# Reciprocal square roots of the norms: one GpSimd power in place of ten VectorE instructions

## The chip, the core and the metric

The kernel runs on one core of a Trainium2 chip. A core has TensorE (matmuls; the trace shows its weight loads apart, as PEld), VectorE (DVE), ScalarE (ACT), GpSimd (POOL) and a sync engine (SP), which here issues nearly all the DMAs. Each engine works through its own instructions in the order in which they stand in the program, and waits on semaphores for the others. The metric is the device time of one execution in microseconds (us).

## What is computed

Two transformer blocks are applied to 256 latent tokens of 1024 features, the second together with 256 context tokens, in float32. Block 1 has an mLSTM branch, a window attention branch and a convolved feed-forward. Block 2 has two layers: layer 0 with an SSD branch and a retention branch for both streams, then a gated feed-forward for both; layer 1 with latent attention over both streams and a feed-forward for the latent tokens. Every layer begins with a norm, and several branches end in one:

```python
def rmsnorm(x, g):
    xf = x.astype(jnp.float32)
    y = xf * lax.rsqrt(jnp.mean(xf * xf, axis=-1, keepdims=True) + EPS)
    return (y * g.astype(jnp.float32)).astype(x.dtype)

# merge of the mLSTM heads
hn = h * lax.rsqrt(jnp.mean(h * h, axis=-1, keepdims=True) + EPS)
```

The change is about the `rsqrt` of these norms alone. What goes into it is small: one number for each token (and for each head, where a norm is over a head).

## The kernel before, in words

Activations lie with the features on the 128 partitions and 256 tokens along the free dimension, so a stream of 1024 features is eight tiles of 128x256. A float32 product is made of three matmuls (`mm3`, lines 289 to 291): each operand is split into a rounded high part and a remainder, and high-high, high-low and low-high are summed in PSUM. The weights come by DMA (`load_w`, line 263); ScalarE makes the high part (`wh`, line 274), VectorE or GpSimd the remainder (`wl`, line 277). GpSimd does it for the lane "f" and for half of the weights of one phase.

There are three lanes: "m" (main), "f" (fill) and "a" (side). Each has its own buffers and PSUM banks, and the lane's letter ends a tile's name: `t_smm` is a tile of small numbers of lane m, `t_wlf` a weight remainder of lane f, `t_ppa` a PSUM bank of lane a. `t_held` is one large tile in which everything that lives long has its columns.

The order of the instructions on each engine isn't the order of the code: a scheduler, which has a cost for every instruction, sets it for the whole program when the program is built. Priorities (`soon`) put some instructions first where they are ready.

A norm over features (`rms_bc`, line 457) goes through four engines. ScalarE squares the eight tiles and VectorE adds them up. TensorE sums over the partitions with a column of ones (line 467), which leaves the sums of 256 tokens as 128x2 in PSUM. VectorE makes mean plus epsilon of it (line 470) and then calls `rsqrt` (line 225). TensorE spreads the result over the partitions by a product with the identity (line 476), and VectorE multiplies the tiles by it (line 520, or 837 at the very end).

`rsqrt` has ten VectorE instructions on a tile of 128x2 or 128x8, each of which needs the one before: an estimate by integer arithmetic on the number's bits (line 229), and three times the Newton step of lines 231, 232 and 233.

It is called 22 times: 15 times by `rms_bc` (128x2), for the merge of the mLSTM heads (128x8; the result is used at line 998 and by the matmul of line 999), for the SSD norm of both streams (128x2; lines 1447 and 1452) and four times for the group norm of the retention heads (128x8; lines 1525 and 1531).

Of the kernel before, what the change touches and what calls it, by code (L numbers as in the profile page):

```python
# [12 lines left out]
I32 = mybir.dt.int32  # L13
# [6 lines left out]
T = 256  # L20
# [4 lines left out]
NKEEP = 5464  # L25
# [23 lines left out]
# ---------------------------------------------------------------- column pack  # L49
# [22 lines left out]
def ap_of(base, dims, spread=0):  # L72
    """The first partitions of base with other free dimensions; spread: on so many partitions the same."""
    part = (0, spread) if spread else tuple(base.ap[0])
    return bass.AP(base.tensor, base.offset, [part] + [tuple(d) for d in dims])


def cl(ap):
    """List of the columns of a [128, n] tile."""
    return [ap[:, i:i + 1] for i in range(ap.shape[-1])]  # L80
# [10 lines left out]
def weave(a, b, na=1, nb=1):  # L91
    """Emit na steps of a, then nb steps of b, and so on, until both are done."""
# [20 lines left out]
def pipelined(first, second, n, ahead=1):  # L113
    """first(0..ahead), then second(i) behind first(i + ahead)."""
# [11 lines left out]
class Lane:  # L126
    """Slots of one strand of work; w: the lane whose weight slots and PSUM banks it uses."""
# [14 lines left out]
    def halves(self, n):  # L142
        """n wide hi/lo blocks, and slots(j) for norm_mod: their j-th halves."""
# [18 lines left out]
class Kern:  # L162
# [12 lines left out]
    # ------------------------------------------------------------ allocation  # L175
# [8 lines left out]
    def soon(self, n=None):  # L184
        """Instructions that go first where they are ready."""
        return self.tc.high_priority(SOON if n is None else n)
# [4 lines left out]
    def keep(self, *shape):  # L191
        """[128, *shape] columns that live to the end."""
# [10 lines left out]
    # ------------------------------------------------------------ constants  # L203
    def setup(self):
# [5 lines left out]
        nc.vector.memset(self.ones, 1.0)  # L210

# [12 lines left out]
    # ------------------------------------------------------------ small math  # L224
    def rsqrt(self, L, v, n, out=None):
        nc = self.nc
        y = out if out is not None else L.sm(n)
        t = L.sm(n)
        nc.vector.tensor_scalar(y.bitcast(I32), v.bitcast(I32), -0.5, float(0x5F3759DF), op0=MUL, op1=ADD)
        for _ in range(3):  # L230
            nc.vector.tensor_mul(t, y, y)
            nc.vector.scalar_tensor_tensor(t, t, -0.5, v, op0=MUL, op1=MUL)
            nc.vector.scalar_tensor_tensor(y, t, 1.5, y, op0=ADD, op1=MUL)
        return y

    def log1p_exp_neg_abs(self, L, x, out, n):
        """out = log(1 + exp(-|x|))"""
# [24 lines left out]
    # ------------------------------------------------------------ weights  # L262
    def load_w(self, L, src, n, unit):
        """Load [128, n] weights; returns w(i) -> (hi, lo) views of the i-th unit columns."""
# [28 lines left out]
    def proj_fm(self, L, W, nk, h, blocks, evac, k0=0, mw=P, lag=1):  # L293
        """Feature-major product: out[m-block][feature, token].  W: [blocks, 128, nk*mw].  evac may return
        a function, which is called behind the products of the lag-th block after."""
# [19 lines left out]
    def proj_tm(self, L, W, nk, n, h, evac):  # L315
        """Token-major product: out[token chunk][token, n].  W: [128, nk*n]."""
# [18 lines left out]
    # ------------------------------------------------------------ adaptive norm parameters  # L335
    def cond_silu(self, name):
        """silu of the conditions, repeated to 32 columns for each feature block."""
# [10 lines left out]
    def ada_first(self, W, cond, bcol, mid, use):  # L348
        """Shift and scale of block 1's mixer, [128, cond, 4] each, handed to use(half of the features, shift, scale)."""
# [25 lines left out]
    def ada(self, W, cond, bcol, out, groups):  # L375
        """out[p, cond, 48]: columns of silu(cond) @ W + b; a group is 8 blocks of 128."""
# [14 lines left out]
    def ada_rows(self, name, n, behind):  # L391
        """silu of n conditions along the free dimension, on every partition; loaded behind a column's writing."""
# [12 lines left out]
    def ada_dve(self, WT, first, rows, blocks, n, bcol, out, pool=lambda i, c: False, behind=lambda: None):  # L405
        """As ada, by rows of the transposed weights, which begin with block first; n(i): conditions of block i;
# [1515 lines left out]
```

## Time and profile before

| | us |
|---|---|
| median of three runs | 1589.98 |
| the three runs | 1586.48, 1589.98, 1597.94 |
| span of the profiled execution | 1588.7 |

Of the profiled execution the profile gives no other time than its span, from its first instruction to its last. That is 1.3 us under the median of the runs. The granted clock is TensorE's clock as the chip let it run, 1.00 being the higher of its two levels (2.4 GHz) and 0.50 the lower (1.2 GHz); its mean over the span is 0.977.

A timeline row gives start, duration, engine, line, operation, output from inputs with their shapes, how many instructions it merges, and in brackets the idle time of the engine before it and what ended it.

### The profile page before, as it was taken

How to read it: one execution, taken by the hardware profiler on the slowest of the kernel's cores; microseconds unless marked ns; L12 is line 12 of the kernel's file. 1: busy time of each engine (PE TensorE's matmuls, PEld its weight loads, DVE VectorE, ACT ScalarE, POOL GpSimd, SP SyncE). 2: the span in 40 equal slices, each digit the busy share in tenths (PEclk: the TensorE clock that was granted, in tenths of full speed). 3: DMA queues.
4: the chain of work that ended last, by engine and by line, in shares of the span. 5: the costliest groups of instructions: out<-in, count | busy, mean ns of one | idle time of the engine just before them, and what ended most of it. 6: DMA issues, size and time to landing. Idle time of an engine off the chain costs nothing.

```text
span 1588.7 us, 28469 instructions
## 1 busy us (share of the span) xinstructions
PE 1509.1 (95%) x10518; PEld 1331.2 (84%) x10518; DVE 1178.0 (74%) x2589; ACT 789.0 (50%) x1703; POOL 371.2 (23%) x350
## 2 busy tenths in 40 slices
PE   6799989999999998998899999999998999999997
PEld 3598876889999987888899888888897875899997
DVE  4367578579999967887875347988677786688786
ACT  3344546565545455644455323322355556566563
POOL 0102125233231163376453101101001112000000
PEclk9799999999999999999899999999999999999999
DMA  9855742446777763334255235687532340255663
GB/s 321 272 184 198 235 160 67 122 171 228 254 237 248 257 209 135 120 98 133 67 161 159 93 110 182 207 281 277 189 120 93 101 152 1 80 178 183 185 186 107
DMA packets 81387, 268.50 MB, mean 169 GB/s; under 512 B 9056, under 2 KB 10720, under 8 KB 80992
## 3 DMA queue, kind: packets, MB, share of 16 engines
q1 hardware_dynamic: 80672, 266.16, 51.5%
q8 instruction: 82, 1.34, 0.3%
q10 hardware_dynamic: 576, 0.52, 0.1%
q14 instruction: 57, 0.47, 0.1%
HBM read 265.60 MB, written 1.05 MB: 168 GB/s over the span
## 4 chain that ended last, share of the span: by engine, by line
PE 81%; DVE 10%; DMA 5%; issue 2%; ACT 2%; POOL 0%; SPq 0%; DVEq 0%; ACTq 0%; POOLq 0%
PE t_ppm L289 18%; PE t_ppm L290 18%; PE t_ppm L291 18%; PE t_ppf L289 4%; PE t_ppf L291 4%; PE t_ppf L290 4%; DVE t_wlm L277 2%; PE t_ppa L431 2%; PE t_ppm L1648 1%; PE t_ppm L1052 1%; DMA t_wra<-in_wada 1%; PE t_ppf L1063 1%; PE t_ppm L1081 1%; DVE t_junk L421 1%; DMA t_wrm<-in_wup 1%
## 5 line engine op out<-in xcount | busy, mean ns | idle before, releaser
L274 ACT CAST t_whm<-t_wrm 128x512 fp32r<-128x512 f32 (+2 forms) x588 | 345.9, 598 | 403.2 <-PE t_ppm L290 282.3
L277 DVE TENSOR_TENSOR t_wlm<-t_wrm,t_whm 128x512 fp32r<-128x512 f32 (+3 forms) x551 | 401.0, 734 | 149.5 <-ACT t_whm L274 137.4
L289 PE MATMUL t_ppm<-t_g1m,t_whm 128*128 128x256 f32 x952 | 271.2, 290 | 2.2 <-ACT t_g1m L526 0.8
L291 PE MATMUL t_ppm<-t_g1m,t_wlm 128*128 128x256 f32 x952 | 267.5, 285 | 3.0 <-DVE t_wlm L277 3.0
L290 PE MATMUL t_ppm<-t_g1m,t_whm 128*128 128x256 f32 x952 | 269.7, 286 | 0.5 <-POOL t_g1m L523 0.5
L289 PEld LDWEIGHTS t_ppm<-t_g1m,t_whm 128*128 128x128 f32 x952 | 181.2, 192 | 7.9 <-issue 3.9
L291 PEld LDWEIGHTS t_ppm<-t_g1m,t_wlm 128*128 128x128 f32 x952 | 181.6, 192 | 5.9 <-DVE t_wlm L277 4.2
L290 PEld LDWEIGHTS t_ppm<-t_g1m,t_whm 128*128 128x128 f32 x952 | 182.7, 192 | 3.2 <-issue 2.1
L277 POOL TENSOR_TENSOR t_wlf<-t_wrf,t_whf 128x512 fp32r<-128x512 f32 (+1 forms) x92 | 121.9, 1337 | 196.0 <-ACT t_whf L274 138.1
L421 DVE SCALAR_TENSOR_TENSOR t_junk<-t_wra,t_sc 128x1024 bf16<-128x1024 f32 x120 | 151.5, 1265 | 16.7 <-DMA t_wra<-in_wada 15.7
L290 PE MATMUL t_ppm<-t_h8m,t_whm 128*128 128x512 f32 (+1 forms) x448 | 159.8, 358 | 1.9 <-DVE t_h8m L529 1.9
L289 PE MATMUL t_ppm<-t_h8m,t_whm 128*128 128x512 f32 (+2 forms) x448 | 159.4, 358 | 1.1 <-ACT t_h8m L528 1.1
L291 PE MATMUL t_ppm<-t_h8m,t_wlm 128*128 128x512 f32 (+1 forms) x448 | 159.9, 358 | 0.0
L274 ACT CAST t_whf<-t_wrf 128x512 fp32r<-128x512 f32 (+2 forms) x148 | 82.8, 573 | 103.3 <-PE t_ppf L290 71.5
L291 PE MATMUL t_ppm<-t_part,t_wlm 128*128 128x258 f32 (+1 forms) x400 | 113.3, 283 | 0.0
L289 PE MATMUL t_ppm<-t_part,t_whm 128*128 128x258 f32 (+1 forms) x400 | 113.0, 283 | 0.0
L290 PE MATMUL t_ppm<-t_part,t_whm 128*128 128x258 f32 (+1 forms) x400 | 112.9, 282 | 0.0
L291 PE MATMUL t_ppm<-t_g2m,t_wlm 128*128 128x256 f32 x352 | 99.1, 284 | 0.4 <-DVE t_wlm L277 0.4
L290 PE MATMUL t_ppm<-t_g2m,t_whm 128*128 128x256 f32 x352 | 99.0, 282 | 0.0
L289 PE MATMUL t_ppm<-t_g2m,t_whm 128*128 128x256 f32 x352 | 99.0, 282 | 0.0
L290 PEld LDWEIGHTS t_ppm<-t_h8m,t_whm 128*128 128x128 f32 x448 | 84.0, 188 | 15.5 <-DVE t_h8m L529 2.3
L289 PEld LDWEIGHTS t_ppm<-t_h8m,t_whm 128*128 128x128 f32 (+1 forms) x448 | 83.5, 188 | 15.0 <-ACT t_h8m L528 1.3
(550 smaller groups left out, 3553.9 us busy)
## 6 DMA issues: line engine op xcount, KB each, us to landing
t_wrm<-in_wup SPq DMA_DIRECT2D x132, 512.0 KB, 4.1
t_wra<-in_wada SPq DMA_DIRECT2D x102, 512.0 KB, 4.9
t_wrm<-in_w_fm SPq DMA_DIRECT2D x30, 512.0 KB, 3.8
t_wra<-in_wada20t SPq DMA_DIRECT2D x24, 512.0 KB, 4.6
t_wrf<-in_w_fm SPq DMA_DIRECT2D x20, 512.0 KB, 5.1
t_wrf<-in_wd SPq DMA_DIRECT2D x24, 384.0 KB, 3.8
t_wrm<-in_win_fm SPq DMA_DIRECT2D x17, 512.0 KB, 3.7
t_wrm<-in_wdown SPq DMA_DIRECT2D x16, 512.0 KB, 4.5
```

The lines of the kernel that those rows point to most:

```text
L274: nc.scalar.copy(hi[:, :c1 - c0], raw[:, c0:c1])
L277: eng.tensor_sub(lo[:, :c1 - c0], raw[:, c0:c1], hi[:, :c1 - c0])
L289: mm(ps, ah, bh, start=start, stop=False)
L290: mm(ps, ah, bl, start=False, stop=False)
L291: mm(ps, al, bh, start=False, stop=stop)
L421: nc.vector.scalar_tensor_tensor(self.tile([P, D], BF16, "junk", 1), raw, 1.0, rows[:, c], op0=MUL, op1=MUL, accum_out=out[:, c, i:i + 1])
L431: self.nc.tensor.matmul(ps[32 * c:32 * c + 32, :T], cond[:, 32 * k:32 * (k + 1)], raw[:, c * T:(c + 1) * T], start=k == 0, stop=k == 7, ti ...
L1052: nc.tensor.transpose(pp[:, j * T + t * P:j * T + (t + 1) * P], Ps[t][:, c * P:(c + 1) * P], self.m["ident"])
L1063: nc.tensor.matmul(po[j * 64:(j + 1) * 64, :T], v[j][c], pts[j][c // 2][:, (c % 2) * T:(c % 2 + 1) * T], start=c == 0, stop=c == 3, tile_p ...
L1081: nc.tensor.matmul(ps, q[:, t * P:(t + 1) * P], kall, start=True, stop=False)
L1648: nc.tensor.matmul(ps, q, K[0:96, hd], start=True, stop=True)
```

## The change

A column block of eight columns of -0.5 is kept (set once by GpSimd), and `rsqrt` becomes one GpSimd `tensor_tensor` with the operation power: `y = v ** -0.5`. Nothing else that is computed changes. Comments and docstrings are taken out of the file as well; with that, a line behind `rsqrt` has a number that is smaller by four in the changed file (476 is 472 there).

```diff
-NKEEP = 5464
+NKEEP = 5472
...
         self.ones = self.keep(P)
         nc.vector.memset(self.ones, 1.0)
+        self.mhalf = self.keep(8)
+        nc.gpsimd.memset(self.mhalf, -0.5)
...
     def rsqrt(self, L, v, n, out=None):
-        nc = self.nc
         y = out if out is not None else L.sm(n)
-        t = L.sm(n)
-        nc.vector.tensor_scalar(y.bitcast(I32), v.bitcast(I32), -0.5, float(0x5F3759DF), op0=MUL, op1=ADD)
-        for _ in range(3):
-            nc.vector.tensor_mul(t, y, y)
-            nc.vector.scalar_tensor_tensor(t, t, -0.5, v, op0=MUL, op1=MUL)
-            nc.vector.scalar_tensor_tensor(y, t, 1.5, y, op0=ADD, op1=MUL)
+        self.nc.gpsimd.tensor_tensor(y, v, self.mhalf[:, :n], op=ALU.pow)
         return y
```

Since the scheduler orders the whole program again, instructions that the diff doesn't touch move too. The first place is TensorE where the latent stream goes from the retention norm and the output product of layer 0 to its feed-forward; it works first for the context stream's norm (lines 467 and 476, in the changed file 463 and 472). Before:

```order
L291 MATMUL t_ppf<-t_g1f,t_wlf 128x256
L467 MATMUL t_ppf<-t_held,t_g1f 128x1
L1511 MATMUL t_ppm<-t_g2m 128x64 x4
L467 MATMUL t_ppf<-t_held,t_g1f 128x1 x3
L476 MATMUL t_ppf<-t_held,t_smf 128x128 x2
L1531 MATMUL t_ppm<-t_held,t_g2m 128x128 x4
L289 MATMUL t_ppm<-t_g1m,t_whm 128x256
```

and now:

```order
L287 MATMUL t_ppf<-t_g1f,t_wlf 128x256
L463 MATMUL t_ppf<-t_held,t_g1f 128x1 x4
L1527 MATMUL t_ppm<-t_held,t_g2m 128x128 x4
L285 MATMUL t_ppm<-t_g1m,t_whm 128x256
...
L287 MATMUL t_ppm<-t_g1m,t_wlm 128x256
L472 MATMUL t_ppf<-t_held,t_smf 128x128 x2
```

The product that spreads the norm's result (472) stood right behind the one that makes its sums, and ahead of the transposes of the retention output (1531, now 1527). It now stands behind the transposes and 24 weight products.

The second place is GpSimd over the same stretch and the norm of the latent stream that follows it, in the changed program (lines 229 are the powers; 273 are weight remainders, 277 before):

```order
L273 TENSOR_TENSOR t_wlf<-t_wrf,t_whf 128x512 x7
L229 TENSOR_TENSOR t_smm<-t_smm,t_held 128x8
L273 TENSOR_TENSOR t_wlf<-t_wrf,t_whf 128x512
L229 TENSOR_TENSOR t_smf<-t_smf,t_held 128x2
L273 TENSOR_TENSOR t_wlm<-t_wrm,t_whm 128x512 x2
L523 TENSOR_TENSOR t_h8m<-t_g1f,t_h8m 128x256 x2
```

The powers stand in GpSimd's one queue among the weight remainders; before, this queue had nothing of the norms' square roots.

The third place is ScalarE where block 1's feed-forward (its gelu at line 820, before 824) overlaps with the SSD branch of the context stream (its exponentials at line 1387, before 1391). Before, one table load stood at the first gelu and the exponentials all ahead of it. Now:

```order
L553 ACTIVATE t_g1m<-t_ppm,t_held 128x256
L820 ACT_TABLE_LOAD
L820 ACTIVATE t_g1m<-t_g1m 128x256
L1389 ACTIVATE t_g2f<-t_held 128x128 x4
L270 CAST t_whm<-t_wrm 128x512
L1387 ACT_TABLE_LOAD
L1387 ACTIVATE t_g2f<-t_ppf 128x512
L270 CAST t_whm<-t_wrm 128x512
L820 ACT_TABLE_LOAD
L820 ACTIVATE t_g1m<-t_g1m 128x256
```

Two exponentials now fall between gelus, so that the table is changed four times more than before (twice here, and twice some 25 rows on).

## Rows read from the trace of the kernel before

**Rows 1.** The page, busy time of each engine, its share, and instructions.

```profile
PE 1509.1 (95%) x10518; PEld 1331.2 (84%) x10518; DVE 1178.0 (74%) x2589; ACT 789.0 (50%) x1703; POOL 371.2 (23%) x350
```

**Rows 2.** The page, chain of work that ended last, by engine.

```profile
PE 81%; DVE 10%; DMA 5%; issue 2%; ACT 2%; POOL 0%; SPq 0%; DVEq 0%; ACTq 0%; POOLq 0%
```

**Rows 3.** Busy times over the span of lines 229, then 233 (instructions in brackets).

```profile
0.00:1588.70 1588.70, 5.77 (x22) 0.98 0.52 169
0.00:1588.70 1588.70, 21.27 (x66) 0.98 0.52 169
```

**Rows 4.** Timeline of TensorE, the products behind a square root.

```profile
221.11 0.46 PE L999 MATMUL t_ppm<-t_g1m,t_g2m 128*128 128x128 f32 x2 [1.76 <-ACT t_g1f L571]
...
730.48 0.46 PE L1452 MATMUL t_ppm<-t_g1m,t_g2m 128*128 128x128 f32 x2 [3.07 <-DVE t_g1m L1447]
...
786.88 1.23 PE L476 MATMUL t_ppf<-t_held,t_smf 128*128 128x128 f32 x4 [2.73 <-DVE t_smf L233]
788.63 1.09 PE L1531 MATMUL t_ppm<-t_held,t_g2m 128*128 128x128 f32 x4 [0.52 <-DVE t_g2m L1525]
...
827.32 1.02 PE L476 MATMUL t_ppm<-t_held,t_smm 128*128 128x128 f32 x4 [2.25 <-DVE t_smm L233]
...
1204.19 0.68 PE L476 MATMUL t_ppf<-t_held,t_smm 128*128 128x128 f32 x4 [2.64 <-ACT t_K L1592]
...
1581.17 0.71 PE L476 MATMUL t_ppm<-t_held,t_smm 128*128 128x128 f32 x4 [2.22 <-DVE t_smm L233]
```

**Rows 5.** Timeline of VectorE, the end of one square root, the last one's input.

```profile
827.10 0.16 DVE L233 SCALAR_TENSOR_TENSOR t_smm<-t_smm 128x2 f32<-128x2 f32 x1
...
1578.99 0.16 DVE L470 TENSOR_SCALAR t_smm<-t_ppm 128x2 f32<-128x2 f32 x1 [1.37 <-PE t_ppm L467]
```

**Rows 6.** GpSimd's instructions by line and shape: count, busy us, mean ns, idle before.

```profile
L277 POOL TENSOR_TENSOR t_wlf<-t_wrf,t_whf 128x512 fp32r<-128x512 f32 x84 | 115.9, 1390 | 156.2 <-ACT t_whf L274 99.0 <-PE t_ppf L291 19.3 <-ACT t_whm L274 16.1
...
L414 POOL COPY t_wra<-t_g1m 128x1 f32<-128x1 f32 x8 | 3.1, 401 | 6.2 <-DVE t_junk L421 3.3 <-issue 2.8
```

**Rows 7.** Timeline of VectorE and GpSimd around an uncovered hand-over between them.

```profile
713.63 0.42 DVE L1423 TENSOR_TENSOR t_g1m<-t_ppm,t_held 128x256 f32<-128x256 f32 x1
...
714.12 0.74 POOL L1425 TENSOR_TENSOR t_g2m<-t_g2m,t_g1m 128x256 f32<-128x256 f32 x1 [1.14 <-DVE t_g1m L1423]
```

**Rows 8.** Timeline of VectorE and GpSimd, at the square roots of rows 4.

```profile
214.43 1.11 DVE L990 TENSOR_SCALAR t_smm<-t_held 128x8 f32<-128x8 f32 x1 [0.62 <-ACT t_g1m L986]
...
214.22 2.71 POOL L277 TENSOR_TENSOR t_wlf<-t_wrf,t_whf 128x512 fp32r<-128x512 f32 x2 [5.87 <-DMA t_wra<-in_wada]
...
723.05 0.17 DVE L1435 TENSOR_SCALAR t_smm<-t_smm 128x2 f32<-128x2 f32 x1 [0.79 <-ACT t_g2m L1433]
...
724.40 2.51 POOL L277 TENSOR_TENSOR t_wlf<-t_wrf,t_whf 128x512 fp32r<-128x512 f32 x2 [2.68 <-ACT t_whf L274]
...
785.57 0.17 DVE L1523 TENSOR_SCALAR t_smm<-t_smm 128x8 f32<-128x8 f32 x1
...
1199.37 0.16 DVE L470 TENSOR_SCALAR t_smm<-t_ppf 128x2 f32<-128x2 f32 x1 [0.25 <-PE t_ppf L467]
```

**Rows 9.** Stretches: from:to, length, busy PE, PEld, DVE, ACT, POOL, granted clock, DMA, GB/s.

```profile
223.40:230.20 6.80, 6.80 (x35) 5.93 (x36) 4.85 (x30) 2.48 (x8) 0.16 (x1) 0.50 0.40 151
732.00:735.40 3.40, 3.40 (x18) 3.40 (x18) 0.31 (x1) 0.98 (x3) 2.52 (x2) 0.50 0.09 37
827.60:831.00 3.40, 3.40 (x18) 3.40 (x18) 2.62 (x7) 1.13 (x3) 0.00 (x0) 0.50 0.27 107
1410.00:1575.00 165.00, 165.00 (x1384) 165.00 (x1383) 128.11 (x257) 101.82 (x190) 12.96 (x10) 1.00 0.58 174
```

**Rows 10.** ScalarE's table load at the gelu, and its high parts of lane m's weights.

```profile
L824 ACT ACT_TABLE_LOAD x1 | 1.3, 1283 | 0.2 <-DVE t_g1m L563 0.2
...
L274 ACT CAST t_whm<-t_wrm 128x512 fp32r<-128x512 f32 (+2 forms) x588 | 345.9, 598 | 403.2 <-PE t_ppm L290 282.3
```

**Rows 11.** Timeline of GpSimd, its first instruction on two tensors.

```profile
32.38 0.72 POOL L527 TENSOR_TENSOR t_g1m<-t_g1m 128x256 fp32r<-128x256 f32 x1 [31.43 <-ACT t_g1m L526]
```

## Prediction

> **What bounds the kernel.** I read the page's busy times first. TensorE is busy for 95% of the span, VectorE for 74%, GpSimd for 23% [rows 1], and of the chain that ended last 81% is TensorE and 10% VectorE [rows 2]. So a VectorE instruction that goes away is worth something only where TensorE stands still for it, and TensorE stands still for 1588.7 - 1509.1 = 79.6 us in all.
>
> Then I asked for the four lines of the square root over the whole span. Line 229 runs 22 times, so there are 22 roots and 220 instructions. Line 233 takes 21.27 us in 66 instructions, a mean of 0.32 us [rows 3], where an undisturbed step takes 0.16 [rows 5]: on average a step is held up as long again. A root is thus at least 10 x 0.16 = 1.6 us long and often several times that.
>
> Third, TensorE's timeline behind each root. At 15 of the 22 TensorE has other work until the root is there. At seven it stands idle just before a product that needs a root; those are the seven rows of [rows 4]: 1.76 us at the mLSTM merge, 3.07 at the latent SSD norm, 2.73 and 0.52 where the context's feed-forward norm and the last retention norm run side by side, 2.25 at the latent feed-forward norm, 2.64 at the first norm of layer 1, 2.22 at the very end. Together 15.2 us: the most that shorter roots can give back directly, 1.0% of the span. (The row at 1204.19 names ScalarE as what it waited for last; the root's chain was the long wait before that.)
>
> Last, the granted clock. After three of these places (the mLSTM merge, the latent SSD norm, the latent feed-forward norm) it falls to 0.50, for 6.8, 3.4 and 3.4 us [rows 9].
>
> **The change, step by step.** *Removed:* 220 VectorE instructions. For 15 roots I cost that at nothing: TensorE's other work hides them, and if that cover goes, what shows is the power's own latency, below.
>
> *Added:* 22 powers on GpSimd. No row shows one. The nearest from below is GpSimd's copy of a single column, 0.401 us; the nearest from above is its subtraction of 512 columns, 1.39 us [rows 6]. A power is more work than a copy, on 2 or 8 columns; I take twice the copy, 0.8 us, for two columns and 1.2 us, most of the way to the upper row, for eight. Nothing in these rows excludes a power that is longer than any of them, and that is the first rival. A hand-over from VectorE to GpSimd costs 714.12 - (713.63 + 0.42) = 0.07 us [rows 7]; from a step's end to TensorE it was 827.32 - 827.26 = 0.06 us [rows 4, 5]. I take 0.07 for each. From the input's start to TensorE's product: 0.16 + 0.07 + 0.8 + 0.07 = 1.1 us.
>
> The Trainium skill (GPSIMD Engine Reference, Engine selection) speaks against the place: element-by-element work belongs on VectorE, since GpSimd is about two times slower on two inputs. The trace agrees in kind, 0.401 us for a copy of one column against 0.16 us for a VectorE step. By that rule alone the power would take some 0.32 us (an estimate: twice that step), still a fifth of ten steps, and the sum below would be 0.5 us lower at the end of the kernel and the same elsewhere.
>
> The seven places:
> - *End.* The sum enters at 1578.99 [rows 5] and the product starts at 1581.17 [rows 4]: 2.18 us become 1.1. Gain 1.1.
> - *First norm of layer 1.* The input is there at 1199.37 + 0.16 [rows 8], the root 0.94 us on, at 1200.5. TensorE's work reached to 1204.19 - 2.64 = 1201.55. Gain 2.6.
> - *Latent feed-forward norm.* TensorE now has 41 rows between the product that makes the sums and the one that spreads the result. A weight product takes 165.00/1384 = 0.119 us [rows 9], so they cover 4.9 us. Gain 2.25.
> - *Latent SSD norm.* Input ready at 723.05 + 0.17; GpSimd idle until 724.40 [rows 8]; root at 724.2, diagonal 0.5 us later. TensorE had work until 730.48 - 3.07 = 727.4. Gain 3.07.
> - *mLSTM merge.* Input at 215.54, GpSimd taken until 216.93 [rows 8], eight columns until 218.2, diagonal until 218.8. TensorE had work until 219.35. Gain 1.76.
> - *Retention norm and context norm.* The mean is there at 785.57 + 0.17 [rows 8]; with 1.2 us of power and 0.7 us for the multiplication behind it, as now, the transposes start at 787.8 in place of 788.63. But the order has moved: the context's spreading product no longer fills part of this wait, it comes 24 products later. So one idle stretch of 3.6 us replaces 2.73 + 0.52. I count 0.
>
> Sum: 1.1 + 2.6 + 2.25 + 3.07 + 1.76 = 10.8 us gained.
>
> *The clock.* At 1.00 a product takes 0.119 us, at 0.50 it took 3.40/18 = 0.189 [rows 9], so 37% of such a stretch is lost. If the three stretches behind gaps that close stay at 1.00, that is 0.37 x 13.6 = 5.0 us. Other idle time of TensorE remains near them; I take 3, with 0 and 5 as bounds.
>
> *Moved, on ScalarE.* Four more table loads of 1.28 us [rows 10], 5.1 us, between casts that TensorE needs. ScalarE waits 403 us in all before these casts, nearly three quarters of it for TensorE to free a buffer [rows 10], so it runs ahead and most is hidden: 0 to 5.1, I take 2. If the cover goes, TensorE waits for the high part of a weight.
>
> *Moved, on GpSimd.* A power can come up while a subtraction of 1.39 us runs [rows 6], or stand behind one whose cast isn't there yet. While the power waits at the queue's head for VectorE, the remainders behind it wait as well, and TensorE for them. And TensorE's cover is thinner: at ten norms 25 to 41 rows now stand between the two products, at an eleventh 15; at nine of these eleven it was more before (up to 61 rows), and 25 rows are 3.0 us. A latency of 1.1 + 1.4 = 2.5 us still fits under that. I take 1.5 us for all of this (0 to 4).
>
> Net: -10.8 - 3 + 2 + 1.5 = -10.3 us, from 1588.7 to 1578.4. The median of the runs is 1.3 us above the profiled span, so the prediction is **1580 us**.
>
> **Rivals.**
>
> *The power is a long routine (slower).* The place is the wait of TensorE's spreading product for GpSimd. For: no row prices a power, and it is unlike the additions and products that GpSimd does here. Against: the tiles have two or eight columns, and even 512 columns of arithmetic take 1.39 us. It decides from about 2.7 us for two columns, where latency passes the 3.0 us of cover. At 5 us, latency 5.3: with 0.119 us a row the eleven norms stand still for 21 us in all, less 5 us of idle time there that two of them had before; the end loses 3 us, the norm of block 1's feed-forward (2 rows of cover) 3, the SSD norm still gains 1.6: +20.4, or 1610 for the median. If eight columns take four times as long, 20 us, the mLSTM merge (root at 216.93 + 20) and the last retention norm lose some 16 and 18 us more: 1644. Chance 0.20, spread over 1592 (at 3 us for either shape) to 1644.
>
> *The new order gives it back (no change).* A whole-program reordering by a table of costs: of TensorE's rows about one in seven stands elsewhere. The bounds above (table loads 5.1, queue 4, clock 0) give -1.7, and a few us of new waits for weights, of the size that are seen now, end at 1585 to 1600. Chance 0.21.
>
> *The clock holds everywhere (faster).* All gains, nothing lost: -10.8 - 5.0, and VectorE, lighter by 220 steps of 0.16 to 0.32 us (35 to 70 us), delivers remainders a little earlier: 1566 to 1574. Chance 0.14.
>
> *The first power waits for code.* GpSimd's first two-input instruction ran at 32.38 [rows 11]; nothing shows that it could have run sooner, and the first norm now needs one earlier. If not, the first norm, its products and the weights behind them shift by up to 18 us, partly under the loads of the start: 1590 to 1608. The Trainium skill (GPSIMD Engine Reference, Instruction dispatch) says that the first call to a freshly loaded kernel pays a load of some 6 us that no instruction shows; by that figure it would be over before the first norm, and no run here shows it yet. Chance 0.05.
>
> **The numbers.** Forecast 0.40 (1574 to 1585). A measurement of this kernel can tell about 1%, 16 us: below 1574 counts as faster, above 1606 as slower. Faster takes the third rival and a little of the forecast's edge: 0.16. Slower takes most of the first rival and a little of the last: 0.20. Within 1%: 0.64. For the range, 1566 to 1612 leaves out the longer half of the slow power and the extreme of the clock case, less than 2 in 10.
>
> **What would show it.** GpSimd rows of line 229, 22 of them, at 0.4 to 1.5 us. The idle time before the spreading products at 1204 and 827 gone, at the end about 1.1 us instead of 2.22; before the transposes of the retention output one gap of about 3.6 us. VectorE's busy time down by 35 to 70 us with TensorE's nearly unchanged. Clock at 1.00 after the latent SSD norm. The prediction is wrong if a power takes over 2.7 us, if GpSimd's queue holds powers back for longer than a subtraction, or if TensorE waits for casts between 340 and 400 us.

## The result, and the profile after

The kernel with the power takes 1575.19 us (median of four runs, 1572.88 to 1576.11), the one before, in runs beside it, 1589.71. The ratio is 0.9896, with a 95% interval from 0.9869 to 0.9922: faster by about 1%, on the border of what the prediction called a change that can be told. The forecast was 1580 with a range from 1566 to 1612. The profiled span went from 1588.7 to 1573.0 us.

First the page of the kernel after, busy times and the chain that ended last. They answer to [rows 1, 2]. Its line numbers are 4 lower than those of before.

```profile
PE 1506.4 (96%) x10518; PEld 1330.7 (85%) x10518; DVE 1133.2 (72%) x2369; ACT 796.1 (51%) x1707; POOL 391.1 (25%) x373
...
PE 78%; DVE 8%; issue 6%; DMA 5%; ACT 2%; POOL 1%; SPq 0%; POOLq 0%; DVEq 0%; ACTq 0%
```

VectorE lost 220 instructions and 45 us. TensorE's work is nearly the same. Its idle time before products, added up from the timeline, fell from 72.8 to 60.1 us; that is 12.7 of the 15.7 us of the span. (The prediction's 79.6 us have the 6.8 us behind the last product as well.)

The new instruction, from GpSimd's groups by line and shape (count, busy us, mean ns, idle before):

```profile
L229 POOL TENSOR_TENSOR t_smm<-t_smm,t_held 128x2 f32<-128x2 f32 x13 | 9.4, 726 | 191.1 <-DVE t_smm L466 185.6 <-DVE t_lgf L242 5.5
L229 POOL TENSOR_TENSOR t_smm<-t_smm,t_held 128x8 f32<-128x8 f32 x3 | 4.9, 1647 | 2.8 <-DVE t_smm L1519 2.5
L229 POOL TENSOR_TENSOR t_smf<-t_smf,t_held 128x8 f32<-128x8 f32 x2 | 3.3, 1638 | 0.0
L229 POOL TENSOR_TENSOR t_smf<-t_smf,t_held 128x2 f32<-128x2 f32 x2 | 1.8, 918 | 0.7 <-DVE t_smf L466 0.7
```

A power of two columns takes 0.70 us where nothing disturbs it, one of eight columns 1.64.

TensorE's timeline at the products that answer to [rows 4] (start, length, line, and in brackets the idle time before and who ended it):

```profile
217.45 0.49 PE L995 MATMUL t_ppm<-t_g1m,t_g2m 128*128 128x128 f32 x2 [0.31 <-DVE t_g1m L994]
...
720.98 0.49 PE L1448 MATMUL t_ppm<-t_g1m,t_g2m 128*128 128x128 f32 x2 [1.56 <-DVE t_g1m L1443]
...
722.21 0.49 PE L1448 MATMUL t_ppm<-t_g1m,t_g2m 128*128 128x128 f32 x2 [0.74 <-DVE t_g1m L1443]
...
775.14 0.83 PE L463 MATMUL t_ppf<-t_held,t_g1f 128*128 128x1 f32 x6 [1.33 <-ACT t_g1f L450]
...
777.90 0.63 PE L1527 MATMUL t_ppm<-t_held,t_g2m 128*128 128x128 f32 x4 [1.93 <-DVE t_g2m L1521]
...
813.01 0.61 PE L472 MATMUL t_ppm<-t_held,t_smm 128*128 128x128 f32 x4
...
1184.90 0.60 PE L472 MATMUL t_ppf<-t_held,t_smm 128*128 128x128 f32 x4
...
1188.16 0.76 PE L285 MATMUL t_ppm<-t_h8m,t_whm 128*128 128x256 f32 x3 [2.66 <-ACT t_h8m L524]
...
1190.80 0.58 PE L286 MATMUL t_ppm<-t_h8m,t_whm 128*128 128x256 f32 x1 [1.88 <-DVE t_h8m L525]
...
1565.81 0.71 PE L472 MATMUL t_ppm<-t_held,t_smm 128*128 128x128 f32 x4 [1.02 <-POOL t_smm L229]
```

The waits at 813 and 1185 are gone, the mLSTM merge waits 0.31 us, the end 1.02. The latent SSD norm still waits 1.56 and 0.74. At the first norm of layer 1 part of the wait has moved on, to the product behind the norm (2.66 and 1.88; it was 1.11 and 1.94 there before).

The granted clock, in stretches of the kernel after (columns as in rows 9):

```profile
608.20:625.30 17.10, 13.59 (x50) 12.00 (x51) 11.63 (x56) 5.53 (x20) 0.00 (x0) 0.50 0.07 27
342.00:345.40 3.40, 3.40 (x10) 1.85 (x9) 3.40 (x8) 3.26 (x7) 1.34 (x1) 0.50 0.85 290
376.10:379.50 3.40, 3.02 (x12) 2.84 (x13) 3.40 (x7) 3.06 (x5) 0.00 (x0) 0.50 0.75 255
778.90:782.30 3.40, 3.40 (x18) 3.40 (x18) 1.30 (x4) 1.52 (x3) 1.07 (x1) 0.50 0.29 117
813.10:816.50 3.40, 3.40 (x31) 3.40 (x30) 2.87 (x8) 2.52 (x7) 3.26 (x3) 1.00 0.51 159
```

0.50 is the lower of the two levels, 1.2 GHz. Behind the latent feed-forward norm the clock now stays at 1.00, as forecast, and so it does behind the mLSTM merge (219.8 to 226.6 us) and the latent SSD norm (722.7 to 726.1). Behind the retention norm (the row at 778.90) half clock went from 10.2 us to 3.4. But other stretches are new or longer: 3.4 us each at 342 and 376 us, at gaps of TensorE that are new, 6.8 us each at 28 and 1284 us, and 17.1 us in place of 6.8 around 615 us. Over the whole span half clock went from 71.6 to 73.9 us.

### The profile page after: what moved, and what is told of

The parts are those of the page before. It is cut to its first block, busy times and chain, and to the rows that moved or that the text cites. A ratio compares the mean times of both kernels' runs of the same rounds, so it can differ in the third digit from the quotient of the medians.

```text
span 1573.0 us, 28294 instructions
## 1 busy us (share of the span) xinstructions
PE 1506.4 (96%) x10518; PEld 1330.7 (85%) x10518; DVE 1133.2 (72%) x2369; ACT 796.1 (51%) x1707; POOL 391.1 (25%) x373
## 4 chain that ended last, share of the span: by engine, by line
PE 78%; DVE 8%; issue 6%; DMA 5%; ACT 2%; POOL 1%; SPq 0%; POOLq 0%; DVEq 0%; ACTq 0%
PE t_ppm L285 17%; PE t_ppm L286 17%; PE t_ppm L287 17%; PE t_ppf L285 4%; PE t_ppf L286 4%; PE t_ppf L287 4%; PE t_ppa L427 2%; PE t_ppm L1644 2%; DVE t_wlm L273 1%; PE t_ppm L1048 1%; PE t_ppf L1059 1%; DMA t_wra<-in_wada 1%; DMA t_wrm<-in_wdown 1%; PE t_ppm L1077 1%; PE t_ppm L972 1%
## 5 line engine op out<-in xcount | busy, mean ns | idle before, releaser
L273 POOL TENSOR_TENSOR t_wlf<-t_wrf,t_whf 128x512 fp32r<-128x512 f32 (+1 forms) x92 | 118.0, 1291 | 193.9 <-ACT t_whf L270 184.2
L287 PE MATMUL t_ppm<-t_h8m,t_wlm 128*128 128x512 f32 (+2 forms) x448 | 159.2, 357 | 0.0
L286 PE MATMUL t_ppm<-t_g2m,t_whm 128*128 128x256 f32 x352 | 98.6, 282 | 0.0
```

The lines of the kernel that those rows point to most:

```text
L273: eng.tensor_sub(lo[:, :c1 - c0], raw[:, c0:c1], hi[:, :c1 - c0])
L286: mm(ps, ah, bl, start=False, stop=False)
L287: mm(ps, al, bh, start=False, stop=stop)
```

## What made a root long

The prediction saw that a step of the old root took 0.32 us on average where an undisturbed one takes 0.16, and left it at that. The reasons stand in the trace of before. This is VectorE's timeline at the latent feed-forward norm, from the input of the root (L470) to the last step but one; the last is in [rows 5].

```profile
819.60 0.16 DVE L470 TENSOR_SCALAR t_smm<-t_ppm 128x2 f32<-128x2 f32 x1 [1.08 <-PE t_ppm L467]
819.79 0.77 DVE L229 TENSOR_SCALAR t_smm<-t_smm 128x2 int32<-128x2 int32 x1
820.60 0.16 DVE L231 TENSOR_TENSOR t_smm<-t_smm 128x2 f32<-128x2 f32 x1
820.80 0.16 DVE L232 SCALAR_TENSOR_TENSOR t_smm<-t_smm 128x2 f32<-128x2 f32 x1
821.00 0.16 DVE L233 SCALAR_TENSOR_TENSOR t_smm<-t_smm 128x2 f32<-128x2 f32 x1
821.07 0.42 DVE L712 SCALAR_TENSOR_TENSOR t_g1f<-t_g1f,t_ppf 128x256 f32<-128x256 f32 x1
821.40 1.27 DVE L231 TENSOR_TENSOR t_smm<-t_smm 128x2 f32<-128x2 f32 x1
822.71 0.67 DVE L232 SCALAR_TENSOR_TENSOR t_smm<-t_smm 128x2 f32<-128x2 f32 x1
823.41 1.21 DVE L233 SCALAR_TENSOR_TENSOR t_smm<-t_smm 128x2 f32<-128x2 f32 x1
824.65 1.20 DVE L231 TENSOR_TENSOR t_smm<-t_smm 128x2 f32<-128x2 f32 x1
825.88 1.18 DVE L232 SCALAR_TENSOR_TENSOR t_smm<-t_smm 128x2 f32<-128x2 f32 x1
```

And GpSimd's in the same stretch:

```profile
817.85 2.69 POOL L277 TENSOR_TENSOR t_wlf<-t_wrf,t_whf 128x512 fp32r<-128x512 f32 x2 [0.26 <-DMA t_wrm<-in_wup]
821.36 1.30 POOL L277 TENSOR_TENSOR t_wlf<-t_wrf,t_whf 128x512 fp32r<-128x512 f32 x1 [0.82 <-ACT t_whf L274]
822.62 0.73 POOL L682 TENSOR_TENSOR t_part<-t_g1f,t_part 128x256 fp32r<-128x256 f32 x1
823.32 3.73 POOL L277 TENSOR_TENSOR t_wlf<-t_wrf,t_whf 128x512 fp32r<-128x512 f32 x3
```

Read the two together. The estimate at 819.79 ends at 820.56, just as the second subtraction of 817.85 ends. Three steps of 0.16 follow while GpSimd rests. The step of 821.40 ends at 822.67, with the subtraction of 821.36; the next ends with GpSimd's addition, and each of the following with one of the three subtractions of 1.24 us. A step that starts while GpSimd works on two tensors waits for the end of GpSimd's instruction. Over the whole span, counted one instruction at a time, 187 of the 220 steps start with GpSimd at rest: they take 0.16 us, and none over 0.17. Of the 33 that start beside a GpSimd instruction, 29 take 0.35 to 1.28 us, and each of these ends 0.02 to 0.03 us after a GpSimd instruction on two tensors. The other four take 0.16: three beside a `MEMSET`, which reads no tensor, and one in the last 0.06 us of a GpSimd product. All waits together are 23.4 us of VectorE. The Trainium skill (SBUF — State Buffer, SBUF: two separate sides) states this: VectorE and GpSimd share one pair of ports under an exclusive lock; a VectorE instruction with two SBUF inputs (against a GpSimd instruction that reads SBUF) or in one of its two-port modes excludes a GpSimd instruction and is excluded by it, and the one that comes second blocks for the whole of the first. The trace agrees for the 25 waiting steps with two inputs and for the three beside a `MEMSET`; four of the 29 are estimates (line 229), which have one input, and no view shows their mode.

GpSimd is not the only cause. VectorE's other instructions stand between the steps in its queue, as the one of line 712 does above. Of the 88.2 us that 21 of the roots took from the input's end to the root's end (all but that of the context's SSD norm), the steps' own 0.16 us make up 33.6, the waits for GpSimd 21.7 and other VectorE instructions about 33. The six roots between 1176 and 1396 us are 27.8 us long and wait for GpSimd for 0.4 us in all.

On GpSimd the root stands in the same queue as the subtractions, so it waits once, for those that stand ahead of it. The same root after:

```profile
808.24 0.16 DVE L466 TENSOR_SCALAR t_smm<-t_ppm 128x2 f32<-128x2 f32 x1 [0.16 <-PE t_ppm L463]
...
810.30 0.69 POOL L229 TENSOR_TENSOR t_smm<-t_smm,t_held 128x2 f32<-128x2 f32 x1
```

It waits 1.9 us, for the rest of one subtraction and the whole of another, and is there 2.6 us after its input, where it was 7.5. From the input's end to the root's end, over all roots but one (that of the context's SSD norm, which ran for 42 us between other work): 88.2 us before, 27.6 after; the median root of two columns 3.85 us before, 0.8 after; of eight columns 5.1 and 1.7. That is some 60 us less; undisturbed (2.0 us against 0.8 and 1.7) they would differ by 21.

## The experiments

All twelve, with the time of each beside the kernel before on the same chip. *Roots* is the sum just told (21 roots, input's end to root's end, from the trace); *middle* is the stretch from the input of the latent SSD root to the product of the latent feed-forward norm, and *its roots* the three roots in it on the latent strand's way (two retention norms, the feed-forward norm). A strand is the work of one stream, here latent or context. These three columns come from one profiled execution of each kernel; the times are medians, and runs of one kernel lie up to 14 us apart (e11).

| kernel | us | ratio, 95% | roots | its roots | middle |
|---|---|---|---|---|---|
| before | 1590 to 1592 | 1 | 88.2 | 17.1 | 104.3 |
| after | 1575.2 | 0.9896 (0.9869 to 0.9922) | 27.6 | 6.0 | 94.8 |
| e1 power in seven | 1587.5 | 0.9974 (0.9959 to 0.9989) | 69.5 | 10.8 | 100.6 |
| e2 power in fifteen | 1585.2 | 0.9960 (0.9945 to 0.9975) | 44.4 | 10.1 | 100.2 |
| e3 one step | 1578.8 | 0.9917 (0.9890 to 0.9944) | 30.1 | 6.5 | 93.4 |
| e4 power twice | 1584.6 | 0.9966 (0.9953 to 0.9980) | 53.0 | 10.1 | 99.9 |
| e5 two steps | 1580.8 | 0.9928 (0.9904 to 0.9952) | 55.8 | 11.9 | 99.2 |
| e6 four steps | 1604.4 | 1.0079 (1.0053 to 1.0105) | 118.3 | 24.3 | 107.8 |
| e7 one root longer | 1591.2 | 1.0006 (0.9986 to 1.0025) | 88.7 | 15.6 | 103.5 |
| e8 exponentials ahead | 1575.3 | 0.9897 (0.9867 to 0.9927) | 27.5 | 6.2 | 94.9 |
| e9 estimate only | 1581.1 | 0.9939 (0.9914 to 0.9965) | 7.2 | 1.8 | 93.8 |
| e10 eights twice | 1588.9 | 0.9993 (0.9978 to 1.0009) | 39.0 | 9.2 | 98.6 |
| e11 eights by Newton | 1587.0 | 0.9973 (0.9950 to 0.9995) | 45.4 | 17.2 | 102.5 |
| e12 power in eights | 1588.5 | 0.9977 (0.9963 to 0.9992) | 70.5 | 10.0 | 99.2 |

**e1 and e2: where the gain sits.** The theory of the prediction (A): only the seven places where TensorE stood idle count.

```diff
+        self.nroot += 1
+        if self.nroot - 1 in (2, 8, 10, 13, 14, 16, 21):   # e2: not in
             self.nc.gpsimd.tensor_tensor(y, v, self.mhalf[:, :n], op=ALU.pow)
+        else:
+            self.newton(L, v, n, y)
```

> The power for the seven roots behind which TensorE stood idle (mLSTM merge, latent SSD norm, last latent retention norm, both feed-forward norms of block 2's layer 0, first latent norm of layer 1, the very end); the ten VectorE steps for the other fifteen. Theory A (the gain is TensorE's idle time behind these seven): nearly all of it stays, 1574 to 1579 us. Rival B (the gain is VectorE's relief, spread over all roots): 7 of 22 of 14.5 us, so 1585. Rival C (the new order as such): no relation to the number, anywhere from 1570 to 1590.

> The reverse: the power for the fifteen roots that TensorE's other work covered, the ten VectorE steps for the seven. Theory A: little gain, 1585 to 1590 us. Rival B: 15 of 22 of 14.5 us, so 1580. Rival C: anywhere from 1570 to 1590.

Measured: 1587.5 and 1585.2. The seven places bring 0.26% (interval 0.11 to 0.41), the fifteen others 0.40% (0.25 to 0.55); which of the two brings more can't be told. A is wrong on e1. In e2 its 1585 to 1590 just holds the 1585.2, but A had the fifteen at next to nothing, and what they bring is clear of noise. B is wrong on e2 (1580); C forecast no number that could fail. TensorE's timeline in e1, at the places and behind them (its lines are 14 higher than after's):

```profile
219.30 0.49 PE L1009 MATMUL t_ppm<-t_g1m,t_g2m 128*128 128x128 f32 x2 [0.33 <-DVE t_g1m L1008]
...
725.45 0.79 PE L1462 MATMUL t_ppm<-t_g1m,t_g2m 128*128 128x128 f32 x2 [3.04 <-DVE t_g1m L1457]
...
777.70 1.44 PE L477 MATMUL t_ppf<-t_held,t_g1f 128*128 128x1 f32 x6 [3.03 <-ACT t_g1f L464]
...
783.10 0.80 PE L299 MATMUL t_ppf<-t_h8m,t_whf 128*128 128x256 f32 x2 [1.20 <-ACT t_h8m L538]
...
786.21 0.58 PE L300 MATMUL t_ppf<-t_h8m,t_whf 128*128 128x256 f32 x1 [2.31 <-DVE t_h8m L539]
...
1575.68 1.22 PE L486 MATMUL t_ppm<-t_held,t_smm 128*128 128x128 f32 x4 [1.02 <-POOL t_smm L231]
```

At the seven places 15.2 us of idle time became 4.4 (0.33, 3.04, 1.02 and nothing at the others): 10.8 us closed, just the sum that was forecast, by coincidence: the latent SSD norm, forecast to close, still waits 3.04, and the retention norm with the context's, put at 0, lost its 3.25. And TensorE's whole idle time fell by 2.0 only, from 72.8 to 70.8. What used to be a wait for the root is now a wait for the tiles before and behind the norm, at 777.70, 783.10 and 786.21. A gap that closes is not a gain by itself.

**e3, e4, e5, e6: the root's length alone.** One, two and four steps in place of three, on VectorE (the edit against the kernel before; e3 is the same, written into the changed file); and the power followed by a second one with exponent 1.

```diff
-        for _ in range(3):
+        for _ in range(1):   # e5: 2, e6: 4
```

```diff
-        self.nc.gpsimd.tensor_tensor(y, v, self.mhalf[:, :n], op=ALU.pow)
+        t = L.sm(n)
+        self.nc.gpsimd.tensor_tensor(t, v, self.mhalf[:, :n], op=ALU.pow)
+        self.nc.gpsimd.tensor_tensor(y, t, self.mone[:, :n], op=ALU.pow)
```

> All roots on VectorE with one Newton step in place of three (4 instructions, less accurate roots), no GpSimd power. Theory A: a root of 4 x 0.16 us, about 0.65 undisturbed, is as short as the power with its hand-overs: 1573 to 1579 us. Rival B: 132 of 220 VectorE instructions go: 60% of 14.5 us, 1581. If only a move to GpSimd helps (VectorE steps are stretched by GpSimd's work): 1582 to 1586.

> Every root as two powers in a row on GpSimd (the second with exponent 1), so 0.7 us longer for two columns and 1.6 for eight, VectorE as in the changed kernel. Theory A: covered roots (eleven with 25 or more rows) show nothing; the end loses 0.7, the last retention norm 1.6, the mLSTM merge 0 to 1.6, the first norm of layer 1 up to 0.7: 1578 to 1581 us. Rival B: VectorE is as light as in the changed kernel, so 1575.

> Two Newton steps in place of three in all 22 roots, all on VectorE, no power (7 instructions per root; the roots are slightly less exact). Theory L (every us that a root is long costs a fixed share, wherever the root stands, since the work that covers it is then missing elsewhere): the time lies on the line through three steps (1591) and one step (1579), so 1585, within 2. Theory S (only the seven places where TensorE stood idle count, 0.5 us each): 1587 to 1588. Theory O (each root length gives another order of the whole program, and the orders differ by several us for no reason of the roots): anything from 1578 to 1596, off the line by more than 3.

> Four Newton steps in place of three in all 22 roots, all on VectorE, no power (13 instructions per root). Theory L: on the same line, 1597, within 2. Theory S: seven places by 0.5 us, 1594 to 1595. Theory O: anything from 1584 to 1602, off the line by more than 3; at or below 1591 would speak for it most plainly.

Measured: 1578.8, 1580.8, 1591 and 1604.4 for one, two, three and four steps; 1584.6 for the power twice. With the steps the time rises, by 2, 10 and 13 us; the 2 are within noise, the other two clear of it. That is no straight line: e5 lies 4 us below L's and e6 7 us above, so L failed in that form, and S (0.5 us at seven places) is far too small for the last two. O had forecast a distance of more than 3 from the line, so an effect of the order stays possible. One step alone, still on VectorE, already has most of the gain; e3 leaves B open (1581 lies in its interval), but e4 doesn't: VectorE is as light there as in the kernel after, and the time is some 10 us longer (0.7%). So the root's length matters, not only the load that VectorE loses. e4 speaks against A and its "nothing" for covered roots as well (1578 to 1581): it makes roots longer by 0.70 us for two columns and 1.64 for eight. It also gives GpSimd some 20 us more work, and no run separates that from the roots' length.

**e7: does an order alone move the time?** One root, where TensorE never waited, gets a fourth step; TensorE's order changes from there on.

```diff
-        for _ in range(3):
+        for _ in range(4 if self.nroot - 1 in (3,) else 3):
```

> The kernel before, with a fourth Newton step in one root alone, that of the norm ahead of block 1's feed-forward, where TensorE did not wait: three more VectorE instructions, 0.5 us, and otherwise the same work; but TensorE's order changes from there on (about a fifth of its rows stand elsewhere). Theory L: 1591 to 1592. Theory S: 1591. Theory O: 3 us or more away from 1591, to either side, which would be the size by which an order alone moves the time.

Measured: 1591.2 beside 1591.1, 0.06% with an interval of 0.2% to either side. Here another order costs nothing that can be seen; its profile still has 3.5 us more idle time of TensorE than before's. This is one other order; what others cost is not shown.

**e8: the four extra table loads.** The context's SSD scores are issued one step ahead, so that no exponential comes between gelus.

```diff
-        yield from pipelined(first, second, 4, 1 if lat else 0)
+        yield from pipelined(first, second, 4, 1 if lat else 1)
```

> The kernel with the power, and the context's SSD scores issued one step ahead of their use (as the latent stream has it already), so that its four exponentials all stand before the first Gelu on ScalarE: three table loads in place of seven, nothing else is computed. If the four loads cost what the prediction took (2 us, bounds 0 and 5.1): 1573, within 1570 and 1575. If the two gaps of TensorE at 339 and 374 us and the two stretches at half clock behind them are all theirs (4.5 us and 2.5 us): 1568. If they are hidden: 1575. Theory O: 3 us or more above 1575 is possible as well.

ScalarE's table loads in the kernel after:

```profile
L820 ACT ACT_TABLE_LOAD x3 | 3.8, 1283 | 2.5 <-DVE t_g1m L559 2.4
L1387 ACT ACT_TABLE_LOAD x2 | 2.6, 1283 | 0.0
```

and in e8 (beside them each kernel has two more, at the start and at the end):

```profile
L820 ACT ACT_TABLE_LOAD x1 | 1.3, 1283 | 2.4 <-DVE t_g1m L559 2.4
```

Two waits of TensorE in this stretch of the kernel after, the second one for an exponential behind a load:

```profile
341.33 1.46 PE L1384 MATMUL t_ppf<-t_g2f,t_held 128*128 128x512 f32 x2 [2.22 <-DVE t_g2f L1381]
...
376.48 1.22 PE L1404 MATMUL t_ppf<-t_g2f 128*128 128x256 f32 x2 [2.31 <-ACT t_g2f L1387]
```

In e8 one wait of 1.28 us is left of the two, neither stretch at half clock is there, and its profiled execution, the fastest of its four runs, is 3.9 us shorter than after's. The medians are 1575.34 and 1575.19, with runs of e8 from 1570.9 to 1579.7. So the loads cost nothing by the medians and some 4 us by the two profiles, which noise alone could make; a version that beats the kernel after isn't shown.

**e9: the integer estimate alone.**

```diff
-        for _ in range(3):
+        for _ in range(0):
```

> The kernel before with no Newton step at all: each root is the integer estimate alone, one VectorE instruction (the three steps that make it exact are left out). From the inputs' ends to the roots' ends the traces so far give, summed over 21 roots (the context's SSD root, which nothing needs at once, left out): 118 us with four steps, 88 before, 56 with two, 53 with the power twice, 30 with one, 28 with one power; the times are 1604, 1591, 1581, 1585, 1579, 1575. Here the sum would be 5 us. Theory L (a fixed share, 0.32 us of time per us of root): 1568, within 3. Theory F (a floor: roots of under 0.8 us are hidden behind TensorE's other products): 1574 to 1576.

Measured: 1581.1, although the roots take 7 us in all. L would have 1568: wrong. A floor (F) is nearer, but its 1574 to 1576 lies below the interval as well (1577 to 1586). Nothing was won here by roots shorter than the power. That they lose against it isn't shown: the intervals of e9 and of the kernel after overlap a little. Nor can the profile say where 6 us would come from, since it is of the fastest of five runs (1575.2; the others 1579.8 to 1581.7) and its span is after's, 1573.0: in it TensorE's idle time is 5.7 us more than after's (65.8 against 60.1) and its busy time 6.1 us less.

**e10, e11, e12: two columns or eight.**

```diff
-        self.nc.gpsimd.tensor_tensor(y, v, self.mhalf[:, :n], op=ALU.pow)
+        if n == 2:   # e12: n == 8
+            self.nc.gpsimd.tensor_tensor(y, v, self.mhalf[:, :n], op=ALU.pow)
+        else:
+            self.newton(L, v, n, y)
```

In e10 the second power of e4 stands behind the five powers of eight columns only.

> The kernel with the power, where the five roots of eight columns are followed by a second power (with exponent 1, so the result stays), and the seventeen of two columns are as they were. The five get longer by 1.64 us and a hand-over each, 8 to 12 us in all. Theory L: 1578 to 1579. If these five are covered (all but the last retention norm have other products beside them): 1575 to 1576. If they are what made the kernel with all powers doubled slow: 1582 to 1585.

> The power for the seventeen roots of two columns, the integer estimate and three Newton steps on VectorE for the five of eight columns. Alone a power of eight columns (1.64 us) is as long as ten VectorE steps; between other VectorE work the ten steps took 5.1 us in the median before. If that is what counts, the five get 13 us longer than with the power: theory L 1579. If only the instructions' own length counts: 1575. If VectorE's lower load is part of the gain: 1576.

> The reverse of the run before: the power for the five roots of eight columns alone (the mLSTM merge and the four retention norms), the estimate and three Newton steps on VectorE for the seventeen of two columns. Over the kernels so far the time goes with the summed length of the eight-column roots (from the input's end to the root's end, 10 us with the power, 24 before, 31 in the run before this) more than with that of the two-column roots (18 and 64): a plane through twelve of them gives 0.64 and 0.14 us of time per us, within 3. Theory E (the eight-column roots are the path, the others mostly covered): 1575 to 1578 if they are all of it, 1583 by that plane. Theory L (length counts alike everywhere, 0.25): 1587. Theory P (gains of parts don't add, since a shorter root in one strand leaves the other strand's in its place): 1585 to 1588, as the other partial kernels.

Measured: 1588.9, 1587.0 and 1588.5. No theory of e10 (1575 to 1585) or of e11 (1575 to 1579) had these times. Five roots of eight columns that are 13.6 us longer in all take back the whole gain (e10); all 22 made longer cost less in e4, though the two profiled spans are the same, 1587.1. Of the 14.1 us between the spans of e10 and after, 9.2 lie ahead of the middle stretch. If the five roots were the path, the power for them alone should bring most of the gain. It brings 3.3 us (e12): E is wrong; P (1585 to 1588) and L (1587) both agree with the interval (1586 to 1591), so neither is shown over the other. The parts don't add: e1 and e2 gain 0.26 and 0.40%, e11 and e12 0.27 and 0.23%, the whole change 1.04%.

**What holds over all of them.** One relation shows in the *middle* columns of the table. In this stretch latent and context strand run side by side, and the latent strand's three roots follow one another. The stretch and the sum of these three roots go together over 14 kernels: a line through them has 0.70 us of stretch per us of root (correlation 0.95, no kernel further off than 2.8 us). Fitted one by one the three roots have 0.74, 0.57 and 0.79, with standard errors of 0.15 to 0.17. The stretch is 9.5 of the 15.7 us between before and after. TensorE in it, before and after (columns as in rows 9):

```profile
723.05:827.32 104.27, 93.30 (x708) 90.46 (x706) 80.78 (x174) 51.44 (x116) 54.24 (x46) 0.93 0.39 123
718.24:813.01 94.77, 88.29 (x700) 86.52 (x700) 70.03 (x123) 49.80 (x114) 57.27 (x49) 0.98 0.40 128
```

Of the 9.5 us 4.5 are idle time of TensorE and 5.0 its products, nearly as many, taking less time: 13.7 us of the stretch stood at half clock before, 3.4 after, which at the prediction's 0.37 is worth 3.8 us (an estimate). So shorter roots go with less waiting here and with a higher clock, and no run takes the two apart.

The first retention root in it is the clearest case. Before:

```profile
766.49 0.17 DVE L1523 TENSOR_SCALAR t_smm<-t_smm 128x8 f32<-128x8 f32 x1
...
767.77 0.16 DVE L229 TENSOR_SCALAR t_smm<-t_smm 128x8 int32<-128x8 int32 x1
...
774.28 0.69 DVE L1525 TENSOR_TENSOR t_g2m<-t_g2m,t_smm 128x512 f32<-128x512 f32 x1
```

and after:

```profile
757.22 0.17 DVE L1519 TENSOR_SCALAR t_smm<-t_smm 128x8 f32<-128x8 f32 x1
757.47 1.65 POOL L229 TENSOR_TENSOR t_smm<-t_smm,t_held 128x8 f32<-128x8 f32 x1 [2.54 <-DVE t_smm L1519]
759.15 1.22 DVE L1521 TENSOR_TENSOR t_g2m<-t_g2m,t_smm 128x512 f32<-128x512 f32 x1
```

Between 766.66 and 774.28 TensorE had no idle time at all, so the prediction put this root down at nothing. It became 5.9 us shorter, and by the fit the stretch gained by it like by the others. That the products of the other strand that covered it were then there to cover the next wait is the likely reading; no run shows it by itself. In the part before this stretch (to 723.1 us before, 718.2 after) the kernels end anywhere from 714.8 to 730.3, with no such line (correlation 0.56 with the roots in it; e9, with the shortest: 719.3), and neither has the part behind it (0.54). The stretch was picked after the traces were seen. What behind it is a length of some root and what the order isn't settled.

## Why the prediction was right, and where it was not

- *The sum* was right in sign, and 5 us short in size (10.3 us of net gain forecast, 15.7 in the spans). That it came so near is in part luck: the seven places brought 6.8 us in place of 10.8 and the clock nothing in place of 3, and what made up for both lies elsewhere, where the prediction had nothing. TensorE's idle time fell by 12.7 us, so by 5.9 outside the seven places. The rivals of a slow power and of a wait for code didn't come, and the new order did not take the gain back.
- *The power.* Two columns: 0.8 forecast, 0.70 measured. Eight: 1.2 forecast with 1.39 as the upper bound, 1.64 measured, above the bound. A small tile isn't a short instruction when the operation is another one than the row's. From the last root's input to its product: 0.99 us against 1.1, as worked out:

```profile
1564.82 0.16 DVE L466 TENSOR_SCALAR t_smm<-t_ppm 128x2 f32<-128x2 f32 x1 [1.37 <-PE t_ppm L463]
...
1565.06 0.69 POOL L229 TENSOR_TENSOR t_smm<-t_smm,t_held 128x2 f32<-128x2 f32 x1 [37.81 <-DVE t_smm L466]
```

- *The seven places.* Forecast 10.8 us. Idle time fell by 1.20 at the end, 2.25 at the latent feed-forward norm, 1.45 at the mLSTM merge; 0.8 of 3.07 at the SSD norm, where the product moved ahead of work that had covered it, and where the two diagonals behind the root (line 1443) took 2.46 us beside GpSimd's subtractions (0.48 before; the forecast had 0.5); 1.2 of 2.64 at layer 1, the rest having moved behind the norm. At the retention norm 1.33 + 1.93 stand where 2.73 + 0.52 stood: the zero was right, though it came as two waits and not as one of 3.6. That makes 6.8 us.
- *The step that failed: fifteen roots at nothing.* Together with the seven as the only place of gain it is the prediction's main assumption. The power in these fifteen alone brings 0.40% (e2), and the stretch in the middle gains by a root that was fully covered. e10 loses everything at five roots, three of them among the fifteen. "TensorE is idle just before the product" tells what ended last, not what the root is worth. In the middle stretch, where one strand covers the other, a us off a root on the latent strand's way went with 0.70 us off the stretch; what the covered roots elsewhere are worth stays open.
- *The held-up steps.* "Held up as long again" was a reading without a reason. With the waits for GpSimd and VectorE's other instructions between the steps it would have been seen that moving the root to GpSimd shortens it by 3 us in the median, not by the 0.5 that lies between ten steps and 1.1 us.
- *The clock.* Forecast 3 us. At the three places named the 13.6 us of half clock are gone, as the prediction had them at best, and at the retention norm 6.8 more; elsewhere half clock rose by 22.7. Over the span it went from 71.6 to 73.9 us: nothing in sum, though the middle stretch gained.
- *Table loads and queue.* 2 and 1.5 us forecast; the loads cost 0 to 4 by e8. In the queue the latent feed-forward root waits 1.9 us, longer than one subtraction (1.26 us there), which the prediction had named as a sign of being wrong; no TensorE wait follows. TensorE does wait between 340 and 400 us, another such sign, but for a VectorE instruction and an exponential and not for casts.
- *The price by rule.* By the Trainium skill (GPSIMD Engine Reference, Engine selection) a power came out at 0.32 us; the trace has 0.70, so the estimate was too low. That GpSimd is the slower engine for such work the trace bears out for one instruction, if of another operation (0.70 us against 0.16 for a step on VectorE); for the root as a whole it came out the other way, since the ten steps on VectorE waited for GpSimd and for VectorE's other work.
- *Code.* The first power starts at 13.77 us, 0.2 us after its input, and takes 0.705 like the others; no wait for code shows. The 6 us that the Trainium skill (GPSIMD Engine Reference, Instruction dispatch) gives for a first load would fit in ahead of it, which no run here separates.

## What to carry to other kernels

When a chain of short VectorE steps takes longer than its steps, look at what GpSimd runs at each step's start, and at what VectorE itself puts between the steps: here one instruction in place of ten escaped most of both. Where two strands cover each other, read a chain's whole length in the trace, input's end to result's end, whether or not the matrix engine is idle at its end; here this held in one stretch, and roots shorter than the power won nothing more. And don't test such a gain by halves: parts of this change gave 0.2 to 0.4% each, the whole 1.0%.

## What the runs showed of the hardware

- GpSimd's power: 0.70 us for 128x2, 1.64 us for 128x8, so about 0.16 us a column over 0.38 (from these two sizes).
- A VectorE instruction of 128x2 that takes 0.16 us took up to 1.28 beside a GpSimd instruction on two tensors. It goes the other way too: two of the 17 powers of two columns took 1.09 and 1.14 us, each started while VectorE worked on two tensors.
- Three VectorE steps that started beside a GpSimd `MEMSET` of 0.31 us took 0.16 us as ever.
